# Layer 1 projection of a DeltaNet trunk: query norms written by POOL, decays scaled on ACT, inversion steps dealt out two per strip

## Chip, cores and metric

One core of a Trainium2 chip runs the whole program in one launch. The metric is the device time in microseconds, the median of the runs. The engines are named PE (TensorE), DVE (VectorE), ACT (ScalarE), POOL (GpSimd) and SP (SyncE, which issues most transfers).

## The reference

A causal decoder trunk of two residual layers on 2048 tokens of 1024 channels. Layer 0 is a pooling and convolution mixer, layer 1 a chunked gated DeltaNet; each is followed by a mixture of 32 experts. The change lies in the first part of layer 1, which from the normalised input `h` makes what the scan over chunks needs. Per head (8 heads of 128 channels, chunks of 64 tokens):

```
u = h @ w_in                                   # q, k, v, z strips, and b, a for the gates
q, k, v = silu(causal_conv4(u))
q, k = l2norm(q), l2norm(k)                    # x * rsqrt(sum(x*x) + EPS); q also * 128 ** -0.5
g = cumsum(gate) within a chunk; decay[i, j] = exp(g_i - g_j) for j <= i
lower = strict_tril((k * beta) @ k.T * decay)
t_mat = inverse(lower + I)                     # 64 x 64, unit lower triangular
a_intra = tril(q @ k.T * decay)
qg, kd = q * exp(g), k * exp(g_last - g)
```

The scan then uses `t_mat`, `a_intra`, `qg`, `kd` and `v`.

## The kernel before, in words

`mixer1` first projects (`dn_project`, to HBM scratch), then scans (`dn_chain`). `dn_project` goes through two halves of 1024 tokens. For each half it normalises and transposes `x` in two chunks of 512 tokens (`norm_T`, tiles `xin`, four buffers), computes the gates, and then calls `dn_head` for 8 heads.

`dn_head` makes four strips of 128 output channels in the order 1, 0, 2, 3 (k, q, v, z). A strip loads its weights, splits them into two fp32r parts (`wh` on ACT, `wl` on DVE, L233 and L234) and runs 48 matmuls into two PSUM tiles (`pm`, L256 to L258). ACT copies them out (`ub`), DVE runs the four-tap convolution (`dacc`, L1208 and L1210), ACT applies silu (`kq` or `vT`). After strips 1, 0, 2 come:
- the transposes of k and q to token-major PSUM (`tk`, L1220), squares on ACT (`sqk`, L1225), sums on DVE (`ssk`, `ssq`, L1227 and L1228);
- `brr` = beta / ssk, `kdf`, and the scaling of the decays `dt` by `brr` on POOL (L1253);
- `nk`, the square root of ssk, by POOL's power (L1257); `kd` on DVE (L1259);
- `fot` = ssq to the power -0.5 on POOL (L1264), then `fo` = `fot` * 128 ** -0.5 on DVE (L1265), which only the scan reads;
- `egb`, a broadcast load of exp(g) (L1267), and `kg` = kq * egb on POOL, 2048 columns (L1269), for which `egb` takes the buffer of `ub`.

Then strip 3, and the products of k and q with k in pairs of token blocks: `kq` is split (`kqh` on ACT, `kql` on DVE), six matmuls per block pair and block (L1281) fill one of two PSUM tiles `tp`, and DVE multiplies them by `dt` into `na` (L1282). So the products of the third pair wait until `na` of the first pair has freed its `tp`. `na` goes to HBM (`stg`, `ndia`, `noff`), the transposes of v make `vp`.

The inversion of 32x32 diagonal blocks runs on DVE for four heads at a time (`dn_invert`, a generator of 31 steps). Step j multiplies j x j columns (`xtmp`, L1312) and sums them (`xblk`, L1313). Its input and result lie in two of the four `xin` buffers, `xtmp` shares one buffer with `sqk`. At the end the result is stored (`xinv`, `xsub`, L1314 and L1318). After each strip `pump(3)` runs the next three steps and one piece of the modulation vectors (`modw`, L168, which ends with the first half). Three inversions are pumped so: heads 0 to 3 of the first half are inverted beside its heads 4 to 7, heads 4 to 7 beside heads 0 to 3 of the second half, and so on; the fourth runs in the scan.

The order on each engine is not the program's order: a planner places instructions by priority (program order) and by modelled readiness, and allots the tile buffers. Each engine then works its list strictly in order.

Of the kernel before, what the change touches and what calls it, by code (L numbers as in the profile page):

```python
# [6 lines left out]
F32 = mybir.dt.float32  # L7
# [3 lines left out]
AF = mybir.ActivationFunctionType  # L11
ALU = mybir.AluOpType
# [4 lines left out]
P = 128  # L17
# [3 lines left out]
EPS = 1e-6  # L21
# [49 lines left out]
class Trunk:  # L71
# [1042 lines left out]
    def dn_project(self):  # L1114
        self.inv = iter(())
        self.stores = []
        tc, nc, ins = self.tc, self.nc, self.ins
        with ExitStack() as ctx:
            ep = lambda name, bufs, **k: ctx.enter_context(tc.tile_pool(name=name, bufs=bufs, **k))
            wp = ep("w1", 2)  # L1120
            hp = ep("h1", 2)
            wk = ep("wk1", 2)
            cv = ep("cv1", 1)
            self.late = ep("late1", 1)
            self.last = ep("last1", 1)
            psm = ep("psm1", 2, space=PSUM)
            psk = ep("psk1", 2, space=PSUM)
            pst = ep("pst1", 2, space=PSUM)
            halo = cv.tile([P, 24, 3], F32, name="halo")
            nc.vector.memset(halo, 0.0)  # L1130
            wba = cv.tile([P, KD, 16], F32, name="wba")
            nc.sync.dma_start(wba, ins["w_ba"])
            wbh = cv.tile([P, KD, 16], F32R, name="wbh")
            wbl = cv.tile([P, KD, 16], F32R, name="wbl")
            self.split(wbh, wbl, wba)

            def xload(c):
                def f(i):
                    t = c * 4 + i
                    x = wk.tile([P, D], F32, name="xin", bufs=4)  # L1140
                    nc.sync.dma_start(x, self.x2[t * P:(t + 1) * P])
                    return x
                return f

            self.rest = self.mod_rest(cv, [(1, i) for i in range(16, 48)], tag="modw", bufs=3)
            for half in range(2):
                hT = []
                ba = cv.tile([P, 8, 16], F32, name="ba", bufs=2)
                for c2 in range(2):
                    hh = hp.tile([P, KD, 512], F32R, name="hh")  # L1150
                    hl = hp.tile([P, KD, 512], F32R, name="hl")
                    self.norm_T(1, 0, xload(half * 2 + c2), pst, wk, (hh, hl))
                    hT.append((hh, hl))
                    p = psm.tile([P, 512], F32, name="pm")
                    self.proj(p[:16], (wbh, wbl), (hh, hl))
                    bs = wk.tile([16, 512], F32, name="bs", bufs=1)
                    nc.scalar.activation(bs, p[:16], AF.Copy)
                    p = pst.tile([P, 512], F32, name="tp")
                    for i in range(4):
                        nc.tensor.transpose(p[:, i * 16:(i + 1) * 16], bs[:, i * P:(i + 1) * P], self.ident[:16, :16])  # L1160
                    nc.vector.tensor_copy(ba[:, c2 * 4:c2 * 4 + 4], p[:, :64].rearrange("p (b c) -> p b c", b=4))
                beta, g, ex = self.gates(half, ba, cv, pst)
                for hd in range(8):
                    self.dn_head(half, hd, hT, beta, g, ex, halo, wp, wk, psm, pst, psk)
                    if hd % 4 == 3 and (half, hd) != (1, 7):
                        self.inv = self.dn_invert(half, hd // 4, wk)

    def pump(self, n):

# [5 lines left out]
    def dn_head(self, half, hd, hT, beta, g, ex, halo, wp, wk, psm, pst, psk):  # L1175
        nc, ins = self.nc, self.ins
        stg = self.stg[half][:, :, hd]
        B8 = lambda t: t[:, hd, :, None].to_broadcast([P, 8, P])
        b8 = lambda t: t[:, :, None].to_broadcast([P, 8, P])
# [8 lines left out]
        def strip(which):  # L1188
            w = self.load_strip(wp, ins["w_in1"][which * 8 + hd], "d")
            if which == 3:  # L1190
                zs = self.last.tile([P, 1024], F32, name="zs", bufs=1)
            else:
                ub = wk.tile([P, 3 + 1024], F32, name="ub", bufs=1)
                si = which * 8 + hd
                nc.gpsimd.tensor_copy(ub[:, 0:3], halo[:, si])
            for c2 in range(2):
                ps = psm.tile([P, 512], F32, name="pm")
                self.proj(ps, w, hT[c2])
                if which == 3:
                    nc.scalar.activation(zs[:, c2 * 512:(c2 + 1) * 512], ps, AF.Silu)  # L1200
                else:
                    nc.scalar.activation(ub[:, 3 + c2 * 512:3 + (c2 + 1) * 512], ps, AF.Copy)
            if which == 3:
                self.stores.append(nc.sync.dma_start(self.zT[half][hd], zs))
                return
            nc.gpsimd.tensor_copy(halo[:, si], ub[:, 1024:1027])
            acc = self.last.tile([P, 1024], F32, name="dacc", bufs=1)
            nc.vector.tensor_scalar(acc, ub[:, 0:1024], self.col("dn_conv", si * 4), None, op0=ALU.mult)  # L1208
            for i in range(1, 4):
                nc.vector.scalar_tensor_tensor(acc, ub[:, i:i + 1024], self.col("dn_conv", si * 4 + i), acc,  # L1210
                                               op0=ALU.mult, op1=ALU.add)
            if which == 2:
                nc.scalar.activation(vT, acc, AF.Silu)
            else:
                nc.scalar.activation(kq[:, :, 1 - which], blk(acc), AF.Silu)

        def tok(src):
            p = psk.tile([P, 1024], F32, name="tk")
            for b in range(8):
                nc.tensor.transpose(p[:, b * P:(b + 1) * P], src(b), self.ident)  # L1220
            return blk(p)

        def sumsq(p, name):
            sq = wk.tile([P, 1024], F32, name="sqk", bufs=1)
            nc.scalar.activation(sq, p.rearrange("p b c -> p (b c)"), AF.Square)  # L1225
            ss = self.small.tile([P, 8], F32, name=name)
            nc.vector.tensor_reduce(ss, blk(sq), axis=AX.X, op=ALU.add)  # L1227
            nc.vector.tensor_scalar(ss, ss, EPS, None, op0=ALU.add)  # L1228
            return ss

        pe = psk.tile([P, 1024], F32, name="tk")
# [7 lines left out]
        dt = self.late.tile([P, 8, P], F32, name="dt", bufs=1)  # L1239
        nc.scalar.activation(dt, blk(pe), AF.Exp)  # L1240
        nc.gpsimd.affine_select(dt, dt, [[0, 8], [1, P]], ALU.is_ge, 0.0, base=0, channel_multiplier=-1)
        strip(1)
        self.pump(3)
        strip(0)
        self.pump(3)
        strip(2)
        self.pump(3)
        pk = tok(lambda b: kq[:, b, 0])
        ssk = sumsq(pk, "ssk")
        brr = self.small.tile([P, 8], F32, name="brr")  # L1250
        nc.vector.reciprocal(brr, ssk)
        nc.vector.tensor_mul(brr, brr, beta[:, hd])
        nc.gpsimd.tensor_mul(dt, dt, b8(brr))  # L1253
        kdf = self.small.tile([P, 8], F32, name="kdf")
        nc.vector.tensor_mul(kdf, brr, ex[:, 1, hd])
        nk = self.small.tile([P, 8], F32, name="nk")
        nc.gpsimd.tensor_tensor(nk, ssk, self.half_.to_broadcast([P, 8]), op=ALU.pow)  # L1257
        kd = wk.tile([P, 8, P], F32, name="kd", bufs=1)
        nc.vector.tensor_mul(kd, pk, b8(kdf))  # L1259
        store(4, 1, kd[:, :, None, :])  # L1260
        pq = tok(lambda b: kq[:, b, 1])
        ssq = sumsq(pq, "ssq")
        fo = self.small.tile([P, 8], F32, name="fot")
        nc.gpsimd.tensor_tensor(fo, ssq, self.expo[:, 0:1].to_broadcast([P, 8]), op=ALU.pow)  # L1264
        nc.vector.tensor_scalar(self.fo[:, hd, half * 8:half * 8 + 8], fo, float(P) ** -0.5, None, op0=ALU.mult)  # L1265
        egb = wk.tile([P, 1024], F32, name="egb", tag="ub", bufs=1)
        nc.sync.dma_start(egb, self.egd[half][hd:hd + 1].to_broadcast([P, 1024]))  # L1267
        kg = self.last.tile([P, 8, 2, P], F32, name="kg", bufs=1)
        nc.gpsimd.tensor_mul(kg, kq, blk(egb)[:, :, None, :].to_broadcast([P, 8, 2, P]))  # L1269
        store(2, 2, kg)  # L1270
        strip(3)
        self.pump(3)
        na = self.last.tile([P, 8, 2, P], F32, name="na", bufs=1)
        for b in range(0, 8, 2):
            p = pst.tile([P, 512], F32, name="tp")
# [10 lines left out]
        for sub in range(4):  # L1286
            dst = bass.AP(tensor=nd.tensor, offset=nd.offset + sub * 32768 + hd % 4 * 1024, ap=[[32, 32], [4096, 8], [1, 32]])
            ss = slice(sub * 32, sub * 32 + 32)
# [399 lines left out]
```

## Time and profile before

| | us |
|---|---|
| median of 3 runs (3411.51 to 3414.04) | 3413.75 |
| the profiled execution | 3413.42 |
| its span | 3411.7 |
| PE busy in the span | 2937.8 (86%) |
| DVE busy in the span | 2482.2 (73%) |
| ACT busy in the span | 1455.1 (43%) |
| POOL busy in the span | 1124.4 (33%) |

The span runs from the first to the last instruction of the one execution that was profiled. The projection of layer 1 lies at about 1310 to 2290 us of it, 16 heads. Times in the rows count from the span's start. The mean TensorE clock granted over the span was 0.927 of full speed.

### The profile page before, as it was taken

To read this page: it belongs to the slowest core of one execution; us is meant where nothing else is said; L and a number is where in the kernel's file an instruction comes from. 1 tells how busy PE (TensorE), PEld (TensorE's weight loads), DVE (VectorE), ACT (ScalarE), POOL (GpSimd) and SP (SyncE) were. 2 spreads that over 40 slices of the span, in tenths; PEclk is the share of its full clock that TensorE was granted. 3 is DMA by queue.
4 is the path that set the end of the run, shared out by engine and by line. 5 is a ranking of instruction groups with operands and counts; after the bars stand their busy time and mean duration, and the time that the engine had idled before them with its cause. 6 is when DMAs were issued, how large, how long until landed. Compare 5 with 4: busy or idle time off the path is not lost. (4 is left out here: it accounts for less than half of the span.)

```text
span 3411.7 us, 41792 instructions
## 1 busy us (share of the span) xinstructions
PE 2937.8 (86%) x14192; PEld 2345.7 (69%) x14192; DVE 2482.2 (73%) x3789; ACT 1455.1 (43%) x2430; POOL 1124.4 (33%) x913
## 2 busy tenths in 40 slices
PE   5979888769999969989888899887897996999991
PEld 3756666547777747777766777777896765777771
DVE  4998998748888856678867867856545556888883
ACT  6134223226565643333333233334663223656552
POOL 1143423333443413242323232235540122344341
PEclk9989989879999989999888999898998997999995
DMA  5216243729999852445442334347767535989875
GB/s 216 91 62 221 77 139 124 247 99 331 297 295 289 274 159 89 138 155 167 153 150 76 102 108 128 102 146 241 220 188 230 180 125 202 310 281 301 268 236 211
DMA packets 384987, 633.40 MB, mean 186 GB/s; under 512 B 111233, under 2 KB 245505, under 8 KB 384769
## 3 DMA queue, kind: packets, MB, share of 16 engines
q1 hardware_dynamic: 355904, 563.38, 48.7%
q0 software_dynamic: 28864, 67.30, 8.5%
q8 instruction: 114, 1.87, 0.2%
q14 instruction: 105, 0.85, 0.1%
HBM read 484.46 MB, written 175.44 MB: 193 GB/s over the span
## 5 line engine op out<-in xcount | busy, mean ns | idle before, releaser
L256 PE MATMUL pm<-hh,wh 128*128 128x512 f32 x1408 | 568.1, 404 | 0.9 <-ACT wh L233 0.7
L257 PE MATMUL pm<-hl,wh 128*128 128x512 f32 x1408 | 557.3, 396 | 4.1 <-DVE hl L229 4.1
L258 PE MATMUL pm<-hh,wl 128*128 128x512 f32 x1408 | 555.7, 395 | 4.3 <-DVE wl L234 4.3
L234 DVE TENSOR_TENSOR wl<-wr,wh 128x1024 fp32r<-128x1024 f32 x384 | 452.0, 1217 | 41.3 <-ACT wh L233 37.8
L233 ACT ACTIVATE wh<-wr 128x1024 fp32r<-128x1024 f32 x384 | 399.4, 1057 | 126.0 <-PE pu L815 57.5
L834 POOL DMA_INDIRECT acc<-ys,ixs x102 | 261.6, 2564 | 435.7 <-DVE wl L234 119.5
L256 PEld LDWEIGHTS pm<-hh,wh 128*128 128x128 f32 x1408 | 270.6, 192 | 63.2 <-issue 4.8
L257 PEld LDWEIGHTS pm<-hl,wh 128*128 128x128 f32 x1408 | 270.4, 192 | 63.4 <-DVE hl L229 4.5
L258 PEld LDWEIGHTS pm<-hh,wl 128*128 128x128 f32 x1408 | 268.8, 191 | 62.5 <-DVE wl L234 5.6
L813 PE MATMUL pu<-wh,xt 128*128 128x512 f32 x656 | 268.3, 409 | 0.5 <-ACT xt L233 0.5
L814 PE MATMUL pu<-wl,xt 128*128 128x512 f32 x656 | 261.1, 398 | 0.0
L815 PE MATMUL pu<-wh,xt 128*128 128x512 f32 x656 | 260.1, 397 | 0.0
L234 DVE TENSOR_TENSOR wl<-wraw,wh 128x1024 fp32r<-128x1024 f32 x88 | 126.3, 1435 | 171.9 <-ACT wh L233 171.7
L282 DVE SCALAR_TENSOR_TENSOR acc<-cin,wfir,acc 128x512 f32<-128x512 f32 (+1 forms) x320 | 214.5, 725 | 0.1
L532 PE MATMUL po<-woh,yh 128*128 128x512 f32 x512 | 172.9, 414 | 31.4 <-issue 11.6
L233 ACT ACTIVATE wh<-wraw 128x1024 fp32r<-128x1024 f32 x88 | 93.2, 1059 | 242.2 <-PE pm L257 242.0
L1210 DVE SCALAR_TENSOR_TENSOR dacc<-ub,cols,dacc 128x1024 f32<-128x1024 f32 x144 | 188.8, 1311 | 2.7
L532 PE MATMUL po<-wol,yh 128*128 128x512 f32 x512 | 166.7, 406 | 0.0
L532 PE MATMUL po<-woh,yl 128*128 128x512 f32 x512 | 165.8, 403 | 0.2 <-DVE yl L234 0.2
L791 POOL DMA_INDIRECT xg<-hn,ixs x102 | 111.3, 1091 | 165.8 <-PE tp L801 80.0
L189 POOL TENSOR_TENSOR rs<-rs1t,expo 128x1 f32<-128x1 f32 x48 | 28.3, 590 | 384.3 <-DVE rs1t L187 327.4
L815 PEld LDWEIGHTS pu<-wh,xt 128*128 128x128 f32 x656 | 123.8, 189 | 30.7 <-DVE xt L234 0.5
(378 smaller groups left out, 6511.3 us busy)
## 6 DMA issues: line engine op xcount, KB each, us to landing
wr<-in_w_up_dram SPq DMA_DIRECT2D x256, 512.0 KB, 7.5
wr<-in_w_down_dram SPq DMA_DIRECT2D x128, 512.0 KB, 7.2
modw<-in_modwT_dram SPq DMA_DIRECT2D x96, 512.0 KB, 5.0
wraw<-in_w_in_dram SPq DMA_DIRECT2D x88, 512.0 KB, 3.6
stin<-stg SPq DMA_DIRECT2D x32, 1280.0 KB, 8.9
yr<-yT SPq DMA_DIRECT2D x32, 512.0 KB, 4.6
acc<-xo SPq DMA_DIRECT2D x32, 512.0 KB, 4.0
hn<-ho SPq DMA_DIRECT2D x32, 512.0 KB, 3.2
```

Source lines behind the costliest of these rows:

```text
L233: a = nc.scalar.activation(h, x, AF.Copy) if eng == "act" else nc.vector.tensor_copy(h, x)
L234: return a, nc.vector.tensor_sub(l, x, h.bitcast(F32))
L256: nc.tensor.matmul(ps, wh[:, k], hh[:, k], start=k == 0, stop=False)
L257: nc.tensor.matmul(ps, wh[:, k], hl[:, k], start=False, stop=False)
L258: nc.tensor.matmul(ps, wl[:, k], hh[:, k], start=False, stop=k == KD - 1)
L282: self.tap = nc.vector.scalar_tensor_tensor(o, x, w, i, op0=ALU.mult, op1=ALU.add)
L532: nc.tensor.matmul(ps[:, ns], a[:, k], b[:, ns], start=k == 0 and i == 0, stop=k == KD - 1 and i == 2)
L813: nc.tensor.matmul(ps, xh[:, k], uh, start=k == 0, stop=False)
L814: nc.tensor.matmul(ps, xh[:, k], ul, start=False, stop=False)
L815: nc.tensor.matmul(ps, xl[:, k], uh, start=False, stop=k == KD - 1)
L834: st = nc.gpsimd.indirect_dma_start(out=self.acc, out_offset=bass.IndirectOffsetOnAxis(ap=ix[:, 0:1], axis=0), in_=ys, in_offset=None, bou ...
L1210: nc.vector.scalar_tensor_tensor(acc, ub[:, i:i + 1024], self.col("dn_conv", si * 4 + i), acc, op0=ALU.mult, op1=ALU.add)
```

## The change

Four edits in `dn_project` and `dn_head`.

```diff
@@ dn_project
-                    if hd % 4 == 3 and (half, hd) != (1, 7):
-                        self.inv = self.dn_invert(half, hd // 4, wk)
+                    if hd % 4 == 3:
+                        assert next(self.inv, None) is None
+                        self.inv = self.dn_invert(half, hd // 4, wk) if (half, hd) != (1, 7) else iter(())
@@ dn_head
-        def sumsq(p, name):
+        def sumsq(p, name, scale=1.0):
...
-            nc.vector.tensor_scalar(ss, ss, EPS, None, op0=ALU.add)
+            nc.vector.tensor_scalar(ss, ss, EPS, scale, op0=ALU.add, op1=ALU.mult)
...
         strip(1)
-        self.pump(3)
+        self.pump(2)
...
-        nc.gpsimd.tensor_mul(dt, dt, b8(brr))
         kdf = self.small.tile([P, 8], F32, name="kdf")
         nc.vector.tensor_mul(kdf, brr, ex[:, 1, hd])
+        for b in range(8):
+            nc.scalar.activation(dt[:, b], dt[:, b], AF.Copy, scale=brr[:, b:b + 1])
...
-        ssq = sumsq(pq, "ssq")
-        fo = self.small.tile([P, 8], F32, name="fot")
-        nc.gpsimd.tensor_tensor(fo, ssq, self.expo[:, 0:1].to_broadcast([P, 8]), op=ALU.pow)
-        nc.vector.tensor_scalar(self.fo[:, hd, half * 8:half * 8 + 8], fo, float(P) ** -0.5, None, op0=ALU.mult)
+        ssq = sumsq(pq, "ssq", float(P))
+        nc.gpsimd.tensor_tensor(self.fo[:, hd, half * 8:half * 8 + 8], ssq, self.expo[:, 0:1].to_broadcast([P, 8]), op=ALU.pow)
```

All four `pump(3)` of a head become `pump(2)`. The power is now taken of 128 * (ssq + EPS), which gives the factor 128 ** -0.5 with it. Sixteen pumps of two steps are 32 calls, and an inversion has 31 steps.

## Rows read from the trace of the kernel before

**Rows 1.** Busy time of each engine in stretches of one head each, from the end of one head's longest PE wait to the next. Columns: the stretch, its length, busy us (and instructions) of PE, PE's weight loads, DVE, ACT and POOL, the granted clock, the share of the DMA engines, GB/s. In order: a plain head of the first half (no inversion), the third head (C) of the first and of the second inversion, the fourth head (D) of the second inversion, called the light head, and the third head (C) of the third inversion.

```profile
1409.71:1467.73 58.02, 52.73 (x245) 44.24 (x245) 40.15 (x47) 19.14 (x24) 20.06 (x15) 0.94 0.46 149
1644.98:1709.85 64.87, 55.12 (x245) 45.85 (x245) 58.72 (x64) 21.21 (x28) 21.48 (x15) 0.89 0.51 168
1926.89:1990.62 63.73, 54.68 (x251) 45.48 (x251) 51.85 (x51) 19.03 (x24) 19.73 (x16) 0.95 0.37 112
1990.62:2046.26 55.64, 52.39 (x244) 43.36 (x245) 32.81 (x35) 19.14 (x24) 19.18 (x16) 0.97 0.36 108
2163.61:2228.37 64.76, 56.61 (x251) 47.00 (x251) 51.51 (x51) 19.14 (x24) 17.98 (x15) 0.90 0.36 111
```

**Rows 2.** Groups of PE instructions by line and shape: busy us, mean ns of one, then the idle time ahead of them and what ended it. The first four rows are the same line in four stretches: 1345 to 1530 (four plain heads), 1530 to 1768 (the four heads beside the first inversion), 1860 to 2050 (beside the second), 2050 to 2232 (three heads beside the third). The last row is of the whole projection, 1310 to 2290.

```profile
L1281 PE MATMUL tp<-kqh 128*128 128x256 f32 x29 | 10.3, 356 | 21.1 <-DVE na L1282 21.1
...
L1281 PE MATMUL tp<-kqh 128*128 128x256 f32 x32 | 11.2, 350 | 23.3 <-DVE na L1282 23.3
...
L1281 PE MATMUL tp<-kqh 128*128 128x256 f32 x28 | 10.1, 361 | 21.6 <-DVE na L1282 21.6
...
L1281 PE MATMUL tp<-kqh 128*128 128x256 f32 x24 | 8.6, 359 | 18.0 <-DVE na L1282 18.0
...
L1220 PE MATMUL tk<-ident,kq 128*128 128x128 f32 x256 | 32.9, 282 | 14.3 <-ACT kq L1215 14.3
```

**Rows 3.** Timeline of DVE, POOL and PE in a plain head. Columns: start, length, engine, line, operation, what it writes and reads, shape, count, and in brackets the idle time ahead of it and what ended it.

```profile
1399.85 1.85 DVE L1255 TENSOR_TENSOR kdf<-brr,gex 128x8 f32<-128x8 f32 x1
1403.30 4.47 DVE L1265 TENSOR_SCALAR fo<-fot 128x8 f32<-128x8 f32 x1 [1.60 <-POOL fot L1264]
...
1410.62 0.68 DVE L1282 TENSOR_TENSOR na<-tp,dt 128x512 f32<-128x512 f32 x1
...
1398.79 2.88 POOL L1253 TENSOR_TENSOR dt<-dt,brr 128x1024 f32<-128x1024 f32 x1 [2.07 <-DVE ssq L1228]
...
1403.24 4.51 POOL L1269 TENSOR_TENSOR kg<-kq,egb 128x2048 f32<-128x2048 f32 x1
...
1409.71 0.56 PE L1281 MATMUL tp<-kqh 128*128 128x256 f32 x1 [5.28 <-DVE na L1282]
```

**Rows 4.** The same view around the wait at the end of the light head (2046.26).

```profile
2039.54 0.17 DVE L1265 TENSOR_SCALAR fo<-fot 128x8 f32<-128x8 f32 x1 [2.09 <-POOL fot L1264]
2040.45 0.69 DVE L1282 TENSOR_TENSOR na<-tp,dt 128x512 f32<-128x512 f32 x1 [0.74 <-PE tp L1281]
2041.06 4.46 DVE L234 TENSOR_TENSOR wl<-wraw,wh 128x1024 fp32r<-128x1024 f32 x1
...
2039.85 4.58 POOL L1269 TENSOR_TENSOR kg<-kq,egb 128x2048 f32<-128x2048 f32 x1 [0.34 <-DMA egb<-egd]
...
2046.26 0.46 PE L1281 MATMUL tp<-kqh 128*128 128x256 f32 x1 [2.99 <-DVE na L1282]
```

**Rows 5.** DVE's timeline in the second head (B) and in the first (A) beside the second inversion; then groups of the inversion's instructions over the projection by shape, as in rows 2: the multiplications of steps 15, 25 and 31, and the sums of steps 25 and 31 (the first and the last of seven steps).

```profile
1918.01 4.48 DVE L1265 TENSOR_SCALAR fo<-fot 128x8 f32<-128x8 f32 x1 [1.64 <-POOL fot L1264]
...
1926.07 1.28 DVE L1282 TENSOR_TENSOR na<-tp,dt 128x512 f32<-128x512 f32 x2
...
1856.80 4.72 DVE L1312 TENSOR_TENSOR xtmp<-xblk,nblk 128x121 f32<-128x121 f32 x1
...
L1312 DVE TENSOR_TENSOR xtmp<-xblk,nblk 128x225 f32<-128x225 f32 x3 | 1.7, 556 | 0.1
...
L1312 DVE TENSOR_TENSOR xtmp<-xblk,nblk 128x625 f32<-128x625 f32 x3 | 4.5, 1493 | 0.0
...
L1312 DVE TENSOR_TENSOR xtmp<-xblk,nblk 128x961 f32<-128x961 f32 x3 | 5.4, 1804 | 0.0
...
L1313 DVE TENSOR_REDUCE xblk<-xtmp 128x25 f32<-128x625 f32 x3 | 2.4, 801 | 0.0
...
L1313 DVE TENSOR_REDUCE xblk<-xtmp 128x31 f32<-128x961 f32 x3 | 3.4, 1148 | 0.0
```

**Rows 6.** ACT's instructions of one line in the scan (min/median/max ns, first and last start), which scale 128x128 by a column; ACT's timeline in the plain head of rows 3; the time from issue to landing of the loads of `egb`, min/median/max us; and the issue of one of them in the B head of rows 5.

```profile
L1498 ACT ACTIVATE on<-ob,fac x128: 384/386/402, 2312.4 to 2568.7; 128x128 f32<-128x128 f32 x128
...
1402.27 1.06 ACT L233 ACTIVATE wh<-wraw 128x1024 fp32r<-128x1024 f32 x1 [2.53 <-PE pm L257]
...
DMA to landing us min/median/max: 3.3/3.7/5.3
...
1913.45 0.33 SPq L1267 DMA_DIRECT2D egb<-egd  x1
```

**Rows 7.** SP's timeline (transfers issued) around the end of the first inversion and at the start of the second half, and PE's at the start of the second half and of the scan.

```profile
1675.82 0.33 SPq L1141 DMA_DIRECT2D xin<-acc  x1
...
1678.41 2.85 SPq L1318 DMA_DIRECT2D xsub<-xblk  x4
...
1683.38 0.33 SPq L1141 DMA_DIRECT2D xin<-acc  x1
...
1779.04 1.77 SPq L1141 DMA_DIRECT2D xin<-acc  x4
...
1770.16 3.67 PE L225 MATMUL tp<-ident,xin 128*128 128x128 f32 x16
...
1789.99 2.58 PE L225 MATMUL tp<-ident,xin 128*128 128x128 f32 x8 [4.87 <-DVE xin L219]
...
2286.81 1.91 PE L1416 MATMUL mm<-xt,na 128*128 128x32 f32 x8 [6.61 <-POOL na L1347]
```

More of the change, by code (lines that the diff above doesn't have):

```diff
@@ L1242, in dn_head @@
         strip(1)
-        self.pump(3)
+        self.pump(2)
         strip(0)
-        self.pump(3)
+        self.pump(2)
         strip(2)
-        self.pump(3)
+        self.pump(2)
         pk = tok(lambda b: kq[:, b, 0])
@@ L1271, in dn_head @@
         strip(3)
-        self.pump(3)
+        self.pump(2)
         na = self.last.tile([P, 8, 2, P], F32, name="na", bufs=1)
```

## The prediction

> **What bounds the kernel now.** I read the busy times by stretch first, one stretch per head of the layer 1 projection, cut where TensorE's largest wait ends [rows 1]. In all of them PE is the busiest engine or next to it, and its busy time hardly moves (52 to 57 us) while the length of a head moves from 55.6 to 64.9 us: PE sets the pace and its idle time is what can be won. Second, the groups of PE instructions with what ended their idle time [rows 2]: nearly all of it is two waits. The first product of k and q of a later block pair (L1281) waited 21.1 + 23.3 + 21.6 + 18.0 = 84.0 us for `na` on DVE, 15 times. The transposes of k (L1220) waited 14.3 us for `kq`, mostly in one head of each of the three inversions, so 4.8 us a time.
>
> Third, the timeline of one plain head [rows 3]. POOL multiplies `kg` from 1403.24 for 4.51 us. DVE starts `fo`, eight columns, at 1403.30, and it takes 4.47 us: it ends with `kg`. `kd`, `na`, `wl` and the second `na` stand behind it in DVE's queue, and PE loses 5.28 us. So the instruction that the change deletes is the one that is held. But fourth, a light head of the second half [rows 4]: there `fo` slipped in ahead of `kg` (0.17 us), the first `na` followed, and now `wl` took 4.46 us beside a `kg` of 4.58 us. The second `na` stood behind `wl`, and PE still lost 2.99 us. In an inversion head the held one was `xtmp` (4.72 us for 121 columns, where 225 take 0.56) [rows 5]. `kg` holds whatever comes, unless it is `na`, which reads PSUM and took 0.69 us beside `kg`.
>
> **The change, part by part.** The sum is made against the profiled execution, 3413.42 us (span 3411.7), 0.33 us under the median of the three runs, 3413.75.
>
> 1. *fo's DVE instruction goes, POOL writes the result.* The power is the same POOL instruction with another address; the factor is folded into a DVE instruction that exists (second operand of ssq's TENSOR_SCALAR), at no new instruction. Taken naively, the whole 84.0 us would return. The light head says otherwise, so I price the four plain heads of the first half by it: 58.02 - 55.64 = 2.38 us per head [rows 1], times 4 = **-9.5**. `kg` could also start earlier, now that `dt` is off POOL, but its input `egb` lands a median 3.7 us after its issue [rows 6], which is close to where `kg` starts now; I count nothing for that (bounds 0 and -0.85 us per head).
>
> On this the Trainium skill speaks against the change ("SBUF — State Buffer", section "SBUF: two separate sides"): VectorE and GpSimd share one port pair as a lock held for a whole instruction, and a VectorE instruction wants it when it has two SBUF inputs or runs in a 2-port mode. By that rule deleting `fo` only hands the wait to `wl`; by the row of `fo` alone the stall would go with it. The trace of the light heads agrees with the rule (4.46 us on `wl`).
>
> 2. *dt's scaling moves from POOL to eight ACT instructions.* Eight of 128x128 with a column as scale take 0.386 us each by `on` of the later stage, and successive ones start closer, so at most 3.1 us [rows 6]. In the plain head ACT is idle 2.53 us between `vT` and `wh` [rows 6], after the scales are known. At worst `wh` is 0.6 us later, and `wl`, which waits for it, stands behind `kg` anyway: 0. Without that cover it costs 0.6 us times 16 = 10. On the gain side POOL's 2.88 us leave, and with them a wait on DVE: `kdf`, eight columns, took 1.85 us beside `dt` [rows 3]. DVE then reaches `kd` earlier, but `na` waits for PE's products, so in plain heads nothing comes of it; in inversion heads it is part of term 3.
>
> 3. *Two inversion steps per strip instead of three.* An inversion has 31 steps; at three per pump it ended at the 11th of 16 pumps, at two it ends at the 16th. Call its four heads A to D. The waits for `na` in the eleven inversion heads followed by another head are 23.3 + 21.6 + 18.0 = 62.9 us [rows 2].
>    - A and B: in the B head of rows 5 `fo` was held from 1918.01 for 4.48 us, two steps followed, then `na` at 1926.07. Without `fo`, step `xtmp` can run ahead of `kg` (`egb` issued at 1913.45, so `kg` about 1917.2), and only one later step is held. Counting down the queue with the new, smaller steps (0.6 + 0.4 us), `na` comes at about 1923.4, 2.6 us earlier; the B gap goes from 7.5 to about 5.0, A to 4.8.
>    - C: it now has steps 23 to 25 ahead of `na`, where before it had none: about 5.5 us of wait instead of 3.5 to 5.4.
>    - D: one step (31) alone, 1.80 + 1.15 us [rows 5], before `kg`: like a light head, 3.0.
>    - Sum: 2 x (4.8 + 5.0 + 5.5 + 3.0) + (4.8 + 5.0 + 5.5) = 51.9, against 62.9: **-11.0**. Bounds: 0 (the steps are pulled forward as now) and -30 (all like light heads).
>    - The transposes' wait: steps 25 to 31 stand between `na` and the convolution that makes the next head's `kq`: seven steps of 2.29 to 2.95 us, about 18.4 us [rows 5]. After the change it is steps 26 to 30 or 25 to 30, 13.2 or 15.6 us, so `kq` comes 5.2 or 2.8 us earlier and a wait of 4.8 goes whole or by 60%. After these waits PE also runs slow for a while, at the lower of its two levels: the mean granted clock in two of these heads is 0.89 and 0.90 against 0.97 in the light one, and PE is busy 55.12, 54.68 and 56.61 us in the three instead of 52.39, 9.2 us together [rows 1]. I take three quarters of 14.3 + 9.2: **-17.6** (bounds -23.5 and -8).
>
> 4. *The inversion ends late.* Its two tiles are two of the four `xin` buffers. Before, the third load of the second half's `xin` was issued at 1675.82, when the last `xtmp` was done with `nblk`, and the fourth at 1683.38, after the stores of the inverse, whose four `xsub` began at 1678.41, so 5 us behind the last step's end [rows 7]. PE used these tiles at 1770.16. After, step 31 is dealt to the strip before that point: by the queue of head D it ends at about 1761, so the fourth load is issued at about 1766. Landing (4 us), ACT's square, POOL's power and DVE's four scalings took 10 us from load to transposes for the second chunk (1779.04 to 1789.99, [rows 7]). So the transposes come at about 1777 instead of 1770: **+7**. PE has nothing else then. Bounds +2 (the head before is shorter, part of the chain overlaps) and +13 (step 31 itself held by `kg`).
>
> 5. *End of the projection.* The third inversion's stores (2.85 us of SP for `xsub`, by the first one's) now come among the first loads of the scan. The first product there waits 6.61 us for a tile of such a load [rows 7]. I take **+2** (0 to +5).
>
> Sum: -9.5 - 11.0 - 17.6 + 7 + 2 = -29.1, so 3413.4 - 29.1 = 3384.3, plus 0.3 to the runs' median: about **3385**.
>
> **The rivals.**
> - *The stall goes altogether*: nothing that has to run beside `kg` is held, or it is not ahead of `na`. All of 84.0 and 23.5 return, less terms 4 and 5: 107.5 - 9 = 98.5 us faster, about 3315. For it: in the plain head nothing but `fo` is held by `kg` [rows 3]. Against it: where `fo` was short, `wl` or `xtmp` was long [rows 4, 5]. Chance 0.08.
> - *The wait only changes its name*: other steps are pulled into the new room, A, B and C come out as before in sum, and the 17.6 is mostly eaten by the late end. About -5, 3409. For it: the steps depend on nothing but each other, and the planner already fills DVE's room ahead of `na` with them. Chance 0.18.
> - *Slower: a step in every strip 3*. Place: the pump just ahead of `na`. So far only A and B have steps there; dealt out evenly, C and D have them too, each with an `xtmp` that meets `kg`. If all inversion heads come out like B (7.5 us), the waits are 11 x 7.5 = 82 instead of 62.9, +19.6, and step 31 held by `kg` makes term 4 +13 and term 5 +5. Against that stand -9.5 and, with the steps pulled forward, -20 at most: +8, about 3421. It decides from the point where the mean wait for `na` in inversion heads is over about 6.8 us. Chance 0.17.
>
> **How the numbers follow.** The forecast, 0.57, has a range of its own of 3362 to 3402. The range for 8 in 10 leaves out the first rival and the upper part of the last: 3338 to 3418. A measurement of this kernel tells 0.2%, 6.8 us, from no change. Faster by more: 0.55 of the forecast, 0.08 and 0.06 of the second rival, together 0.69. Slower by more: 0.15 of the last and 0.02 of the second, 0.17. The rest, 0.14, is the same.
>
> **What would show it.** Term 1: plain heads of 55 to 56 us, and `wl` or another instruction with two SBUF inputs of over 4 us beside each `kg`; if none is long, the first rival holds. Term 2: eight short `dt` instructions per head on ACT, and `wh` not later than now against PE. Term 3: no wait of PE for `kq` over 2 us, and a mean wait for `na` of 4.5 to 5 us in inversion heads; over 6.8 the slower rival holds. Term 4: PE idle some 7 us ahead of the second half's first transposes, released by `xin`. The prediction is wrong in its main step if the order of DVE's queue around `kg` is another than today's: it is planned anew, and the steps are what the planner moves most easily.

## The result, and the profile after

The changed kernel takes 3396.98 us (median of 5 runs, 3394.08 to 3397.64) where the kernel before takes 3413.75 (5 runs, 3411.51 to 3415.81): 16.8 us less, a ratio of 0.995 [0.9936, 0.9965]. The forecast was 3385, so the sign and the range were right and the size was 12 us off. The page of the changed kernel begins so:

```profile
span 3395.2 us, 41934 instructions
...
PE 2939.8 (87%) x14192; PEld 2344.0 (69%) x14192; DVE 2472.0 (73%) x3773; ACT 1492.9 (44%) x2558; POOL 1112.1 (33%) x897
```

PE is as busy as before (2937.8 us), so the 16.5 us that the span lost were idle time of PE. The groups of PE instructions of the changed kernel over the layer 1 projection (columns as in [rows 2]; line numbers have moved by one) show which:

```profile
L256 PE MATMUL pm<-hh,wh 128*128 128x512 f32 x1013 | 402.6, 397 | 3.8 <-ACT ub L1203 3.8
...
L1281 PE MATMUL tp<-kqh 128*128 128x256 f32 x128 | 46.6, 364 | 61.4 <-DVE na L1282 61.4
...
L1221 PE MATMUL tk<-ident,kq 128*128 128x128 f32 x256 | 31.5, 276 | 7.5 <-ACT kq L1216 7.5
...
L225 PE MATMUL tp<-ident,xin 128*128 128x128 f32 x64 | 14.7, 369 | 21.4 <-DVE xin L219 20.0 <-ACT nf L227 1.4
```

Two waits of [rows 2] shrank: that for `na` from 84.0 to 61.4, that for `kq` from 14.3 to 7.5. Two others grew: that for `xin` on DVE by 15.1 us (before 4.9, nearly all of it the 4.87 of [rows 7]), that for `ub` on ACT by 3.6 (before 0.2). Together -22.6 - 6.8 + 15.1 + 3.6 = -10.7 us.

The same account in order of time, as the lead of the changed kernel over the one before at points that both traces have (start of an instruction on the span's clock):

| point | before | after | lead |
|---|---|---|---|
| first gate product of the projection | 1306.98 | 1304.46 | 2.5 |
| end of a plain head's wait for `na` | 1409.71 | 1403.11 | 6.6 |
| last wait for `na` of the first half | 1767.32 | 1748.19 | 19.1 |
| first transposes of the second half | 1770.16 | 1765.44 | 4.7 |
| last transposes there | 1800.84 | 1798.80 | 2.0 |
| last but one head, end of its wait for `na` | 2228.37 | 2212.12 | 16.3 |
| first product of the scan | 2286.81 | 2273.53 | 13.3 |
| end of the span | 3411.7 | 3395.2 | 16.5 |

So the lead grew to 19 us in the first half, fell by 14 to the first transposes at the seam of the halves and by 17 to the last ones, and grew by 14 again. Of the whole, 2.5 us lie ahead of the projection and 3.2 in the scan, in code that the diff doesn't touch; the runs of the kernel before differ by 4.3 us among themselves, so these 5.7 us can't be put down to anything.

**The hold in a plain head.** The timeline of the changed kernel, the head of [rows 3]:

```profile
1397.49 0.69 DVE L1282 TENSOR_TENSOR na<-tp,dt 128x512 f32<-128x512 f32 x1 [1.92 <-PE tp L1281]
1398.10 4.27 DVE L234 TENSOR_TENSOR wl<-wraw,wh 128x1024 fp32r<-128x1024 f32 x1
1402.29 0.68 DVE L1282 TENSOR_TENSOR na<-tp,dt 128x512 f32<-128x512 f32 x1
...
1396.70 4.58 POOL L1269 TENSOR_TENSOR kg<-kq,egb 128x2048 f32<-128x2048 f32 x1 [1.06 <-DMA egb<-egd]
...
1393.87 2.43 ACT L1257 ACTIVATE dt<-dt,brr 128x128 f32<-128x128 f32 x8
1396.50 1.06 ACT L233 ACTIVATE wh<-wraw 128x1024 fp32r<-128x1024 f32 x1 [0.20 <-PE pm L257]
...
1403.11 0.55 PE L1281 MATMUL tp<-kqh 128*128 128x256 f32 x1 [2.85 <-DVE na L1282]
```

`fo` is gone, the first `na` goes through beside `kg`, and now `wl` is held: it starts 1.4 us into `kg` and ends 1.1 us behind it. The second `na` stands behind `wl`, and PE waits 2.85 us where it waited 5.28. Eight `dt` take 2.43 us on ACT, and `wh` follows without being late.

**The seam of the halves.** SP's transfers and PE's first transposes in the changed kernel:

```profile
1739.98 0.33 SPq L1141 DMA_DIRECT2D xin<-acc  x1
1741.17 0.32 SPq L1314 DMA_DIRECT2D xinv<-xblk  x1
...
1746.38 0.37 SPq L1184 DMA_DIRECT2D stg<-kg  x1
1747.43 4.09 SPq L1318 DMA_DIRECT2D xsub<-xblk  x4
1751.95 0.38 SPq L1184 DMA_DIRECT2D stg<-na  x1
...
1757.46 0.58 SPq L1141 DMA_DIRECT2D xin<-acc  x1
...
1765.44 0.66 PE L225 MATMUL tp<-ident,xin 128*128 128x128 f32 x2 [14.24 <-DVE xin L219]
```

The inversion is done by 1741, but SP works its list in order: the store of `kg` stands ahead of `xsub`, and the stores of `na` and `vp` ahead of the fourth `xin` load, which is issued at 1757.46 (1683.38 before, [rows 7]). PE stands 14.24 us. That costs twice: the stretch behind the wait also runs at a low granted clock. The stretch from the last wait of the first half to the last transposes at the seam, first of the kernel before, then of the changed one (columns as in [rows 1]):

```profile
1767.32:1800.84 33.52, 25.29 (x115) 15.70 (x116) 14.92 (x24) 22.35 (x37) 1.01 (x1) 0.76 0.50 170
```

```profile
1748.19:1798.80 50.61, 27.48 (x114) 17.25 (x115) 17.83 (x29) 23.61 (x39) 2.01 (x2) 0.64 0.39 132
```

For 115 and 114 matmuls, PE was busy 25.29 us at a granted clock of 0.76 before, 27.48 us at 0.64 after. The stretch as a whole is 17.1 us longer.

### The profile page after: what moved, and what is told of

The parts are those of the page before. It is cut to its first block, busy times and chain, and to the rows that moved or that the text cites. A ratio compares the mean times of both kernels' runs of the same rounds, so it can differ in the third digit from the quotient of the medians.

```text
span 3395.2 us, 41934 instructions
## 1 busy us (share of the span) xinstructions
PE 2939.8 (87%) x14192; PEld 2344.0 (69%) x14192; DVE 2472.0 (73%) x3773; ACT 1492.9 (44%) x2558; POOL 1112.1 (33%) x897
## 5 line engine op out<-in xcount | busy, mean ns | idle before, releaser
L233 ACT ACTIVATE wh<-wr 128x1024 fp32r<-128x1024 f32 x384 | 399.4, 1057 | 126.2 <-PE pu L815 56.5
L234 DVE TENSOR_TENSOR wl<-wraw,wh 128x1024 fp32r<-128x1024 f32 x88 | 133.8, 1520 | 186.6 <-ACT wh L233 186.6
```

Of the source, the lines that this page charges most:

```text
L233: a = nc.scalar.activation(h, x, AF.Copy) if eng == "act" else nc.vector.tensor_copy(h, x)
L234: return a, nc.vector.tensor_sub(l, x, h.bitcast(F32))
```

## The experiments

Each kernel was timed beside the kernel before on the same chip, whose median was 3411.59 to 3415.19 in the four groups of runs. Ratios are to the kernel before of the same group. "Wait for `na`" is that of the group of the first products (84.0 before, 61.4 after). The theory: `kg` on POOL holds what runs beside it on DVE, the edits choose what that is and whether an `na` stands behind it; and the late end of the inversion takes back half of what is won. In these traces the held ones are `wl`, `xtmp` and `mod`, which have two SBUF inputs, but also `fo` and `rst` (4.47 us each), which have one beside constants; why these two are among them was not tested apart. `na`, which reads PSUM, and the sums `xblk` are not held.

### The query norms alone

Only the new `sumsq` argument and the power written by POOL, on the kernel before:

```diff
-        ssq = sumsq(pq, "ssq")
+        ssq = sumsq(pq, "ssq", float(P))
...
-        nc.vector.tensor_scalar(self.fo[:, hd, half * 8:half * 8 + 8], fo, float(P) ** -0.5, None, op0=ALU.mult)
```

> The kernel before with the query-norm edit alone (POOL writes fo, factor folded into ssq); decays still scaled on POOL, three inversion steps per pump. Theory (kg's multiplication holds any DVE instruction with two SBUF inputs; without fo it holds wl or xtmp): plain heads fall from 58.0 to 55.5 to 56 us, wl or xtmp of over 4 us beside every kg, total 3396 to 3405. Rival (the stall belongs to fo): waits of PE for na under 1 us, total under 3345. Rival (the gain of the changed kernel came from the decays' move): plain heads stay at 58.0, total 3414.

3392.24 us (3386.41 to 3395.03), 0.9936 [0.9922, 0.995]: 22.3 us faster, 4 more than the most that was expected. This one edit brings what the three bring together, or more. From its trace, DVE, POOL and PE in a plain head, and the group of the first products:

```profile
1399.86 4.99 DVE L234 TENSOR_TENSOR wl<-wraw,wh 128x1024 fp32r<-128x1024 f32 x1
...
1399.22 4.55 POOL L1267 TENSOR_TENSOR kg<-kq,egb 128x2048 f32<-128x2048 f32 x1
...
1405.60 0.55 PE L1279 MATMUL tp<-kqh 128*128 128x256 f32 x1 [3.58 <-DVE na L1280]
```

```profile
L1279 PE MATMUL tp<-kqh 128*128 128x256 f32 x128 | 45.7, 357 | 58.2 <-DVE na L1280 58.2
```

`wl` takes the place of `fo`, as in the light head of [rows 4], and PE's waits in plain heads are 3.6 us instead of 5.3. From one such wait to the next a plain head takes 56.5 us in the mean, against 58.0 before and 55.7 in the changed kernel. The wait for `na` falls by 25.8 us.

### The decays on ACT alone

```diff
-        nc.gpsimd.tensor_mul(dt, dt, b8(brr))
+        for b in range(8):
+            nc.scalar.activation(dt[:, b], dt[:, b], AF.Copy, scale=brr[:, b:b + 1])
```

> The kernel before with the decays scaled on ACT alone; fo stays a DVE instruction behind POOL's power. Theory: with dt's 2.9 us off POOL the power is done, and so fo runs, about a microsecond before egb lands and kg starts; so fo is not held, wl is, and plain heads fall to 55.5 to 56 us as with the other edit alone; total 3396 to 3405. The two edits would then be two ways to the same gain and not add up. Rival (moving the scaling only swaps engines): plain heads 58.0, total 3412 to 3416.

3398.32 us (3396.28 to 3399.42), 0.9954 [0.9941, 0.9968]: 16.2 us faster, as this theory had it. DVE and POOL in a plain head of its trace, then the groups of `fo` and of the first products:

```profile
1399.83 0.17 DVE L1266 TENSOR_SCALAR fo<-fot 128x8 f32<-128x8 f32 x1 [1.44 <-POOL fot L1265]
...
1402.26 4.36 DVE L234 TENSOR_TENSOR wl<-wraw,wh 128x1024 fp32r<-128x1024 f32 x1
...
1400.97 4.57 POOL L1270 TENSOR_TENSOR kg<-kq,egb 128x2048 f32<-128x2048 f32 x1 [1.17 <-DMA egb<-egd]
```

```profile
L1266 DVE TENSOR_SCALAR fo<-fot 128x8 f32<-128x8 f32 x16 | 2.7, 172 | 18.2 <-POOL fot L1265 18.2
```

```profile
L1282 PE MATMUL tp<-kqh 128*128 128x256 f32 x128 | 46.0, 359 | 68.8 <-DVE na L1283 68.6
```

`fo` is still there, sixteen times, and none is held: 172 ns in the mean, against 2428 ns in the kernel before. Without `dt` POOL is through with `fot` before `egb` has landed, `kg` waits 1.17 us for that load, and `fo` slips in ahead of `kg`; the one that is held in a plain head is `wl`. This edit reaches by the order of the work what the other reaches by deletion. In the sum of the prediction it stands at nothing.

### The two together

Both edits above, with three steps a pump as before:

```diff
-        nc.gpsimd.tensor_mul(dt, dt, b8(brr))
+        for b in range(8):
+            nc.scalar.activation(dt[:, b], dt[:, b], AF.Copy, scale=brr[:, b:b + 1])
...
-        ssq = sumsq(pq, "ssq")
+        ssq = sumsq(pq, "ssq", float(P))
```

> The kernel before with the query-norm edit and the decays' move, three steps per pump as before. Theory: either edit alone already takes fo out of kg's way (3392 and 3398 us), so together they give hardly more than the better of the two: 3386 to 3394, and the pump edit then costs the changed kernel 3 to 11 us net, since it pays 14 us at the start of the second half. Rival (the gains add): 22 + 16 us, 3374 to 3379.

3390.11 us (3385.97 to 3391.48), 0.9929 [0.9916, 0.9943]: 23.5 us, not the 38.5 of the sum. Both edits win the same stall. The changed kernel, which is this one with the third edit, is 6.9 us slower (3396.98, and no run of the one reaches a run of the other): in the change as a whole the new dealing of the inversion steps costs time. The group of the first products, with three steps a pump:

```profile
L1280 PE MATMUL tp<-kqh 128*128 128x256 f32 x128 | 45.9, 358 | 54.9 <-DVE na L1281 54.7
```

So the wait for `na` is 6.5 us shorter here than in the changed kernel: what that one saves on it comes from the first two edits, and the dealing gives some of it back. The dealing wins 6.6 us of the wait for `kq` (14.1 here, 7.5 there) and pays 15.1 at the seam (a wait for `xin` of 4.9 here, 20.0 there) and 3.8 for `ub` (none here).

### The inversion steps alone

All four pumps of a head, and with them the inversion that ends with its sixteenth pump, on the kernel before:

```diff
-        self.pump(3)
+        self.pump(2)
```

> The kernel before with two inversion steps per pump alone. Theory: the wait of PE for kq shrinks (14.3 to about 7 us), but C and D heads get steps ahead of na (3 to 5 us more per inversion), and the late end of the first inversion holds back the second half's first transposes by some 14 us: total 3412 to 3428. Rival (an even spread is a gain by itself): 3395 to 3405.

3447.07 us (3445.42 to 3451.8), 1.01 [1.0085, 1.0115]: 32.5 us slower, far outside what was expected. Two groups of PE instructions, and PE at the start of the second half:

```profile
L1282 PE MATMUL tp<-kqh 128*128 128x256 f32 x120 | 42.8, 357 | 100.1 <-DVE na L1283 100.1
...
L225 PE MATMUL tp<-ident,xin 128*128 128x128 f32 x64 | 14.4, 363 | 23.3 <-DVE xin L219 21.9 <-ACT nf L227 1.4
```

```profile
1791.08 2.58 PE L225 MATMUL tp<-ident,xin 128*128 128x128 f32 x8 [16.80 <-DVE xin L219]
```

The wait for `na` grows by 16 us, with 6.9 to 7.5 us in every inversion head: that is the mechanism of the prediction's slower rival, while `fo` is still there to be held. And the second half's transposes come at 1791.08 instead of 1770.16 [rows 7].

### The late end taken away

Of sixteen pumps of two, the last one runs step 31. One more step in the first pump puts every later step one place ahead, so that step 31 runs in the fifteenth, one strip sooner. First on the changed kernel:

```diff
         strip(1)
-        self.pump(2)
+        self.pump(3 if hd % 4 == 0 else 2)
```

> The changed kernel with three steps instead of two at one pump per inversion (after strip 1 of its first head), so that step 31 no longer is alone in the last pump. Theory (the 14.2 us that PE waits for xin at the start of the second half are the two xin buffers that the inversion holds until its last store): the inversion ends about 45 us earlier, that wait goes, and the total falls by 10 to 15 us to 3382 to 3387. Rival (the transposes are late for another reason, SP's or ACT's order): wait and total stay, 3395 to 3399.

3380.06 us (3379.62 to 3380.65), 0.9901 [0.9886, 0.9916]: 16.9 us under the changed kernel, by one step more in the first pump of each inversion. The groups of the two waits:

```profile
L225 PE MATMUL tp<-ident,xin 128*128 128x128 f32 x64 | 13.0, 343 | 6.8 <-DVE xin L219 5.9 <-ACT nf L227 0.9
```

```profile
L1281 PE MATMUL tp<-kqh 128*128 128x256 f32 x128 | 46.2, 361 | 62.6 <-DVE na L1282 62.6
```

The wait for `xin` is 14.1 us less, that for `na` as before the edit. So the seam is what ate the gain: the edit won back 16.9 us, and the seam had lost 17.1 by the table of leads, up to its last transposes. (Of the smaller waits, that for `ub` goes, 3.8 us, and that for `kq` grows by 2.6.) The same edit on the kernel that has only the new dealing:

> The kernel before with two steps per pump and three at the first pump of each inversion, with neither of the other edits. Splits the 32 us that the pump edit alone cost. Theory: the late end cost 14 to 17 us at the start of the second half and about 7 us at the start of the scan, so 3422 to 3428 remain, over before by the longer waits for na in C and D heads (3 to 4 us each) while fo is still in the way. Rival (all of the cost is the late end): 3410 to 3416.

3418.06 us (3414.16 to 3421.13, 11 runs), 1.0015 [1.0006, 1.0024]: 6.5 us slower than before, between the two theories' numbers. Of the 32.5 us of the new dealing alone, about 26 were the late end. What is left shows in the wait for `na`, which is still 96.4 us:

```profile
L1282 PE MATMUL tp<-kqh 128*128 128x256 f32 x128 | 46.5, 363 | 96.4 <-DVE na L1283 96.4
```

And the kernel of the norms' edit and this dealing, with `dt` left on POOL, so the earlier step's kernel with one edit undone:

```diff
+        nc.gpsimd.tensor_mul(dt, dt, b8(brr))
-        for b in range(8):
-            nc.scalar.activation(dt[:, b], dt[:, b], AF.Copy, scale=brr[:, b:b + 1])
```

> The query-norm edit and two steps per pump with three at the first pump of each inversion; decays on POOL as before. Tells what the decays' move is worth beside the better dealing of steps (3380 us with it). Theory: with dt back on POOL, DVE's small two-input instructions wait up to 2 us for it and kg starts later, once the steps stand there too: 3384 to 3394. Rival (the move does nothing): 3378 to 3382.

3390.93 us (3384.78 to 3396.43), 0.9927 [0.9914, 0.9941]. Against 3380.06 with `dt` on ACT the move of the decays is worth some 10 us here (10.9 by the medians, 9 by the ratios), beside the better dealing; the runs of this kernel lie 12 us apart, but none of them reaches one of the other. Beside three steps a pump it was 2 us (3392.24 to 3390.11), within the spread of the runs.

### No step ahead of the products

On the changed kernel the eight steps of a head go to strips 1, 0 and 2 alone:

```diff
         strip(1)
-        self.pump(2)
+        self.pump(3)
...
         strip(0)
-        self.pump(2)
+        self.pump(3)
...
         strip(3)
-        self.pump(2)
+        self.pump(0)
```

> The changed kernel with three inversion steps after each of strips 1, 0 and 2's share of two, and none after strip 3 (3, 3, 2, 0 instead of 2, 2, 2, 2). Theory (the planner pulls steps forward into DVE's room ahead of na wherever they are dealt, since xtmp's buffer, shared with sqk, is the only bar; what counts is that the inversion's last step falls before its last head): as with three at the first pump, waits for na of 4 to 5 us in inversion heads, no long wait for xin, total 3377 to 3387. Rival (the place ahead of na counts): waits for na near 3 us in inversion heads, total 3350 to 3368.

3376.46 us (3374.91 to 3380.34), 0.9899 [0.9884, 0.9914]: half a microsecond under the theory's lower end. The waits are those of the theory too:

```profile
L1281 PE MATMUL tp<-kqh 128*128 128x256 f32 x128 | 45.5, 355 | 64.1 <-DVE na L1282 64.0
```

With no step dealt to strip 3 the heads A to C still wait 4.3 to 5.75 us for `na`: in eight of these nine heads an `xtmp` of 4.35 to 5.13 us stands beside `kg`, in the ninth a `mod` of 4.22. The three dealings of the changed kernel (61.4, 62.6 and 64.1 us) hardly differ in this wait, though three steps a pump did (54.9); they differ in others (that for `kq` is 3.2 us here, 10.1 with the earlier step). While `kg` runs for 4.5 us, something is held in all of them.

### kg in pieces

That leads to the length of `kg` itself. The product is cut along its eight token blocks:

```diff
-        nc.gpsimd.tensor_mul(kg, kq, blk(egb)[:, :, None, :].to_broadcast([P, 8, 2, P]))
+        for b in range(0, 8, 2):
+            nc.gpsimd.tensor_mul(kg[:, b:b + 2], kq[:, b:b + 2], blk(egb)[:, b:b + 2, None, :].to_broadcast([P, 2, 2, P]))
```

On the kernel before, none of the three edits in it:

> The kernel before, whole, with only kg's multiplication cut into four POOL instructions of 512 columns. Theory (POOL and DVE exclude each other for one instruction at a time): fo, wl or xtmp wait for at most one piece, about 1.2 us, PE's waits for na fall from 84 to 20 to 40 us, and the total to 3345 to 3375, more than the whole change gave. Rival (DVE gets no turn between two pieces of POOL): fo still takes over 4 us in plain heads, total 3405 to 3416.

3376.21 us (3367.56 to 3377.41), 0.9882 [0.9867, 0.9897]: 37.4 us faster, more than twice the whole change, though a microsecond short of the theory, and the wait for `na` fell less than expected:

```profile
L1265 DVE TENSOR_SCALAR fo<-fot 128x8 f32<-128x8 f32 x16 | 14.1, 881 | 28.6 <-POOL fot L1264 28.6
...
L1270 POOL TENSOR_TENSOR kg<-kq,egb 128x512 f32<-128x512 f32 x64 | 99.4, 1582 | 2.2 <-DMA egb<-egd 2.1
```

```profile
L1282 PE MATMUL tp<-kqh 128*128 128x256 f32 x128 | 42.9, 335 | 45.0 <-DVE na L1283 45.0
```

`fo` takes 0.88 us in the mean instead of 2.43: it is held for one piece at most, and then gets its turn. For that POOL pays: a quarter of `kg` would be 4557 / 4 = 1139 ns, and takes 1582. On the changed kernel with the earlier step:

> The changed kernel with three steps at the first pump of each inversion and kg cut into four. Theory: on top of 3380 us the waits for na lose 2 to 3 us in each head, 30 to 45 us: 3335 to 3352. Rival (no turn between pieces): 3377 to 3384.

3341.58 us (3338.74 to 3347.45), 0.9786 [0.9772, 0.9799], inside the theory's range. Wait for `na` 20.6 us. And with no step in strip 3, in four pieces and in eight (step 1 and width 1 in the loop):

> The changed kernel with the steps dealt 3, 3, 2, 0 and kg cut into four: the two best parts together. Theory (their gains lie in different waits): 35 to 39 us under the same dealing with a whole kg (3376), so 3335 to 3342. Rival (with the hold gone, the place of the steps decides): under 3330, or over 3345.

> The same with kg cut into eight pieces of 256 columns. Theory: by four pieces the wait for na is already down to 1.5 to 2 us, and each further piece costs POOL's start; 3332 to 3342, within 5 us of four pieces. Rival (every halving of the piece brings the same again): 3320 to 3328.

3334.84 us (3333.3 to 3338.19), 0.9768 [0.9755, 0.9781], and 3334.56 (3325.27 to 3337.75), 0.9766 [0.9753, 0.9779]: the fastest versions, 80 us under the kernel before, and the number of pieces beyond four makes no difference that the spread of the runs would show. The groups of the products and the timeline of a plain head, four pieces:

```profile
L1282 PE MATMUL tp<-kqh 128*128 128x256 f32 x128 | 40.1, 313 | 17.6 <-DVE na L1283 17.4
L1282 PE MATMUL tp<-kql,kqh 128*128 128x256 f32 x128 | 41.9, 327 | 13.4 <-DVE kql L234 13.1
```

```profile
1396.74 0.69 DVE L1283 TENSOR_TENSOR na<-tp,dt 128x512 f32<-128x512 f32 x1 [1.92 <-PE tp L1282]
1397.35 2.13 DVE L234 TENSOR_TENSOR wl<-wraw,wh 128x1024 fp32r<-128x1024 f32 x1
1399.40 0.68 DVE L1283 TENSOR_TENSOR na<-tp,dt 128x512 f32<-128x512 f32 x1
...
1395.86 6.44 POOL L1270 TENSOR_TENSOR kg<-kq,egb 128x512 f32<-128x512 f32 x4 [0.96 <-DMA egb<-egd]
...
1400.22 0.36 PE L1282 MATMUL tp<-kqh 128*128 128x256 f32 x1 [0.72 <-DVE na L1283]
```

`wl` takes 2.13 us beside `kg` instead of 4.27, and PE waits 0.72 us for `na` instead of 2.85. `kg` takes 6.44 us instead of 4.58, and nothing on PE waits for it. Part of the wait has changed its name once more: the products behind wait 13.4 us for `kql`, which now runs beside the last pieces (1.2 in the changed kernel). With eight pieces that is 3.4 us, and PE waits 12.4 for `ub` instead (5.6 with four), which fits that the two are equally fast.

## Why the prediction was right, and where its sizes were not

- **Term 1, fo's deletion: -9.5, measured -10.1, and not by the deletion alone.** The waits for `na` of the four plain heads went from 21.1 to 11.0 us. That `wl` takes the hold over, as in the light head of [rows 4], was right. But with the deletion alone these waits are 14.4 us and a plain head is 1.6 us shorter, not 2.38; the other 0.8 comes with the decays' edit, by which `kg` starts earlier. I had named that as a bound (0.85 per head) and counted nothing for it, so that the term came out is in part luck. The Trainium skill's lock, held for a whole instruction ("SBUF — State Buffer", section "SBUF: two separate sides"), spoke for a hold that passes on, and the traces here agree, `wl` at 4.27 and 4.99 us most directly; cutting `kg` is the test that the hold lasts as long as POOL's one instruction.
- **Term 2, dt on ACT: 0. No cost, as forecast, but a gain that I did not count.** `wh` was not delayed, as forecast. But I counted no gain in plain heads, because `na` waits for PE there. I had not seen that `dt` on POOL also holds up `fot` and so puts `fo` behind the start of `kg`. Alone the edit wins 16 us; beside the other edit with three steps a pump, 2 us; beside the earlier step, some 10.
- **Term 3, waits for na in inversion heads: -11.0, measured -12.5.** From 62.9 to 50.4 us, 18.3, 17.5 and 14.6 for the three inversions, a mean of 4.6. This is not the dealing's work: with the two other edits and three steps a pump the same waits are 43.7 us, so it added 6.7, mostly in the C heads, as the term had it for them. The slower rival decided from 6.8 us, and that is not reached, because `fo` and `dt` no longer stand in the way: with the dealing alone it is 6.9 to 7.5 in every such head, and that kernel stays 6.5 us slower than before when its late end is taken out. So the rival was a true mechanism, which the two other edits of the same change disarmed.
- **Term 3, wait for kq and the clock behind it: -17.6. This is a step that failed.** The wait fell by 6.8 us, and 3.6 us more of a wait of PE for `ub` on ACT stand against it, so 3.2 net. The sign that I had named, no wait for `kq` over 2 us, did not come: 4.13 and 3.34 us are left. Nor was the slow clock gone, it had moved. The stretches of the changed kernel, as in [rows 1], for head D of the first inversion, then C and D of the second:

```profile
1684.08:1748.19 64.11, 55.69 (x249) 46.44 (x249) 52.23 (x53) 22.52 (x34) 13.68 (x10) 0.90 0.39 122
...
1916.19:1973.41 57.22, 52.52 (x244) 44.36 (x245) 42.64 (x46) 21.48 (x32) 18.71 (x14) 0.95 0.34 108
...
1973.41:2034.86 61.45, 56.40 (x253) 46.88 (x253) 50.22 (x49) 21.36 (x32) 20.54 (x15) 0.92 0.36 115
```

  In the second inversion head C fell from 63.73 to 57.22 us, as the term wanted, and head D, the light head of [rows 1], rose from 55.64 to 61.45, with PE busy 56.40 us instead of 52.39. I gave the term to the heads that lose steps and left out that those which get them would pay it. The wait for `ub` is the late convolution under another name. In that head D, DVE works steps 26 to 30 from 1980.36 to 1994.58 and only then the convolution `dacc`; ACT's list has `kq`, which needs `dacc`, ahead of the `ub` that PE needs:

```profile
1996.30 3.92 DVE L1211 SCALAR_TENSOR_TENSOR dacc<-ub,cols,dacc 128x1024 f32<-128x1024 f32 x3
...
2000.30 1.28 ACT L1216 ACT_TABLE_LOAD   x1 [9.02 <-DVE dacc L1211]
...
2002.55 0.58 ACT L1203 ACTIVATE ub<-pm 128x512 f32<-128x512 f32 x1
...
2003.18 0.80 PE L256 MATMUL pm<-hh,wh 128*128 128x512 f32 x1 [2.38 <-ACT ub L1203]
```

  The 3.34 us for `kq` in the head behind it have another cause: there `dacc` was done at 2057.69, and `kq` began at 2063.22, behind a `wh` on ACT that had waited for PE. What set that order was not tried.
- **Term 4, the late end: +7 (bounds +2 to +13), measured +14.4.** The mechanism was the one described, and the size was over the upper bound. I let the fourth load follow the inverse's last step by 5 us, as in [rows 7]. Here the stores of `kg`, `na` and `vp` stood in SP's queue among the inverse's, and 16.3 us lie between `xinv` and that load; from the load to the transposes it was 8.0 us, where the prediction has 11. Up to the last transposes, with the slow stretch behind the wait, the seam lost 17.1. The earlier step, which takes this term out, made the kernel 16.9 us faster.
- **Term 5, the scan's start: +2, not shown.** The lead fell by 3.0 us up to there, from 16.3 to 13.3, but that stretch holds head D of the third inversion, with 1.39 us of the wait for `ub`, which is in term 3. The scan's first product waits 6.40 us for a load, no longer than before (6.61).

```profile
2273.53 0.85 PE L1416 MATMUL mm<-xt,na 128*128 128x32 f32 x3 [6.40 <-DMA nd<-stg]
```

- **The sum.** By PE's waits the terms are -10.1 - 12.5 - 3.2 + 15.1 (the wait for `xin`) = -10.7, which is what the leads inside the projection say (-10.8); 5.7 us lie outside it. The two misses are term 3's second half (14.4 us) and term 4 (8.1); without the 5.7 us that nobody forecast the time would have been some 3403. Taken by edits the miss lies in one of them. The first two together won 23.5 us, which is what the sum has for them if the A and B heads of term 3, from 43.4 us to 29.4, are put down to `fo` with term 1 (-9.5 - 14.0). The rest of the sum, for the dealing, is -5.6, and the dealing cost 6.9: there the prediction had even the sign wrong, and the sign of the whole came from the other two. Of the rivals, "the stall goes altogether" falls with the 61.4 us that are left, and "the wait only changes its name" holds for a half: the edits of the norms and of the decays renamed a wait, and renamed it to a shorter one.

## What to carry to other kernels

When one engine's instruction holds another's, look at the holder before the held: deleting the held one won 22 us here, moving its neighbour 16, and both together 23.5, while cutting the holder into four won 37 alone and 38 to 42 on top of the better versions. When work is dealt out evenly, ask which buffer the last piece gives back, and read the in-order queue of the transfers between that piece and the next load: dealing one step sooner, so that the last one ended a strip earlier, was worth 17 us. And price an edit with its neighbours in place, since the same move of `dt` was worth 16, 2 and some 10 us beside three sets of others.

## What the runs showed of the hardware that was not expected

- The hold passes instruction by instruction, in both directions. Pieces of `kg` of 512 columns took 1582 to 1727 ns in the mean where a quarter of the whole is 1139 to 1154, and pieces of 256 columns 988 ns where an eighth is 577, so `kg` as a whole grew from 73.9 us in the changed kernel to 108.7 and 122.1, by the groups of the two fastest kernels, four pieces and then eight:

```profile
L1270 POOL TENSOR_TENSOR kg<-kq,egb 128x512 f32<-128x512 f32 x64 | 108.7, 1727 | 22.4 <-DMA egb<-egd 22.3
```

```profile
L1270 POOL TENSOR_TENSOR kg<-kq,egb 128x256 f32<-128x256 f32 x128 | 122.1, 988 | 22.3 <-DMA egb<-egd 22.3
```

  Not all of that is waiting. The shortest pieces took 1268 ns (four) and 716 ns (eight), so 0.11 to 0.14 us a piece over the equal share, an estimate of the price of cutting; the longest of the four-piece kernel took 2449 ns:

```profile
L1270 POOL TENSOR_TENSOR kg<-kq,egb x64: 1268/1726/2449, 1343.0 to 2199.6; 128x512 f32<-128x512 f32 x64
```

  The two kernels are equally fast, so where PE sets the pace a slower POOL is a fair price for a shorter hold.
- Eight scalings of 128x128 on ACT took 2.43 us together, 0.30 each, where the record of a single one is 0.386 long in the scan [rows 6] and 0.387 here: successive ones overlap.
